# An adaLN gate loaded one group earlier, and its product parted from the residual sum

## The chip, the cores and the metric

The kernel runs on one core of a Trainium2 chip. The metric is the time of one execution on the device in microseconds (us), taken as the median of several runs. Five engines work side by side, each through an instruction list of its own, in order: TensorE (PE, with its weight loads as PEld), VectorE (DVE), ScalarE (ACT), GpSimd (POOL) and SyncE (SP), whose list here issues nearly all DMA transfers. An instruction that needs another engine's result waits on a semaphore, and what stands behind it on its engine waits with it.

## The reference, cut to what matters

Two layers work on 1024 latent tokens of 1024 features; 256 context tokens go through the first layer with the same weights. Everything is float32.

```python
for i in range(DEPTH):                                   # DEPTH = 2
    with_ctx = i < DEPTH - 1
    h, gate_lat = modulate(x, norm_gain[i], cond_lat @ w_mod[i] + b_mod[i])
    hc, gate_ctx = modulate(xc, norm_gain[i], cond_ctx @ w_mod[i] + b_mod[i])
    ...                                                  # h @ w_in[i], four branches: mlp, ret, ga, swa
    if with_ctx:
        xc = xc + gate_ctx * (jnp.concatenate([mlp_c, ret_c, ga_c, swa_c], axis=-1) @ w_out[i])
    x = x + gate_lat * (jnp.concatenate([mlp_l, ret_l, ga_l, swa_l], axis=-1) @ w_out[i])
```

The change concerns the last two lines: the gate is one value per feature, the same for all tokens, and it multiplies the projected result before that is added to `x` or `xc`.

## The kernel before

**Tiling.** The tokens are ten tiles of 128 (eight of latents, two of context, tiles 8 and 9), and two neighbours make a pair: pairs 0 to 3 are latents, pair 4 is context. Weights come in groups of 256 columns: thirteen input groups per layer for the branches (`GROUPS`, the last is `ua1`), then four output groups for the residual. Each operand of these products is held as a rounded high part and a remainder, and a product is three matmuls (`TERMS`). `HT` holds the operand of all ten tiles, eight blocks of 128 features each.

**From branches to projection.** In `ua_group` (L1216) with p = 1, the last branch group, two things fill `HT` for the projection. `stash_mixed` (L1494) loads the stored results of the other branches into room of the attention pool, and `split_mixed` (L1484) turns each tile's part into high part (ACT, L1491) and remainder (L1492, on DVE, or on POOL for blocks 4 to 6 of odd tiles). The group's own result, block 7, goes the same way chunk by chunk (chunks are tiles 0 to 3, 4 to 7, and 8 and 9): two activation steps end in `ge` and `sl` (DVE, each in a `gv` buffer), L1244 multiplies them, POOL multiplies by the stored `svl` (L1249), and a split follows.

**Projection and residual.** `project` (L1533) runs four groups of 256 output columns (n = 0 to 3). For each group it computes one unit per pair (`unit_a`, L418): 48 matmuls over tile and k, the blocks 0 to 7, into one of two PSUM buffers (`pj`). Pairs come in the order 4, 0, 1, 2, 3 in layer 0, and 0 to 3 in layer 1. Behind each unit `residual` (L1583) does three things on DVE and ACT: the gate product `tm` (L1587) from PSUM, the sum into `xr` (L1589), and in layer 0 the squares for the next norm; in layer 1 the sum is stored to the output. `residual` gives back both the PSUM buffer and the `gv` buffer that holds the product.

**The residual's room.** `x` and the gate rows lie in a pool that takes the place of the attention pool. `enter` (L1539) opens it once every buffer of the attention pool is free, that is, behind the last split of the stash; it queues the DMAs: the first 256 columns of the gate and of `x`, and 8 us later by the planner's clock the rest. A gate load (L1552) spreads one row of DRAM over 128 partitions.

**What sets the order.** The instruction lists are written by a planner when the kernel is built (`later`, `hook`, `fits`, L276 to L329). A step is queued with the time at which its inputs should be there by a rough model of the engines; what it needs is a number of buffers by tag and a condition. Whenever the main loop has issued a few matmuls, `hook` runs the steps that are due and fit, earliest first. A step queued by another one is due when the work of that one ends in the model. So the place of an instruction in its engine's list depends on modelled times, on the buffers, and on the condition. The tags that matter are `gv` (4 buffers), `pj` (2) and `vf` (1). `vf` holds the values of an attention group, and in the retention groups `dec`, the decay table (L692), which `Bb1`, the group before `ua1`, reads last (L1401).

The line that ties the product to the pool, in `project`:

```python
self.residual(l, n, pair, tiles, ps, XR[pair], gb[c], None if last else room[pair]), "gv", lambda: XR)
```

Its last argument is the condition: `XR` is an empty list until `enter` has run.

Of the kernel before, what the change touches and what calls it, by code (L numbers as in the profile page):

```python
# [12 lines left out]
F32 = mybir.dt.float32  # L13
# [177 lines left out]
class Program:  # L191
# [161 lines left out]
    def room(self, need):  # L353
        self.until(lambda: self.fits([(need, 1)], None))
# [861 lines left out]
    def ua_group(self, W, p):  # L1216
        V, G, l = self.V, self.G, self.l
        svs = {}

        def load_sv(t0, w):  # L1220
            sv = self.tile(self.gp, (128, 512), F32, "M", "svl")
            self.SP.dma_start(out=sv[:, :w], in_=self.svd[l][p, :, 128 * t0:128 * t0 + w])
            svs[t0] = sv

        if p == 1:
            for ch in self.order():
                t0, n = CHUNKS[ch]
                self.later(lambda t0=t0, w=128 * n: load_sv(t0, w), "M", lambda t0=t0, n=n: all(("v", l, t // 2) in self.made for t in range(t0, t0 + n)))
            stash = self.stash_mixed()
        for ch in self.order():  # L1230
            t0, n = CHUNKS[ch]
            w = 128 * n
            box = {}

            def got(which, a, box=box, t0=t0, n=n, w=w):
                box[which] = a
                if len(box) == 2:
                    if p == 0:
                        self.later(lambda: load_sv(t0, w), "M", lambda: all(("v", l, t // 2) in self.made for t in range(t0, t0 + n)))
                    self.later(lambda: both(box, t0, n, w), "", lambda: t0 in svs)  # L1240

            def both(box, t0, n, w):
                m, g = box["u"], box["g"]
                V.scalar_tensor_tensor(m[:, :w], m[:, :w], 0.25, g[:, :w], ALU.mult, ALU.mult)  # L1244
                self.done(g)
                self.later(lambda: fin(m, svs.pop(t0), t0, n, w))

            def fin(m, sv, t0, n, w):
                G.tensor_mul(m[:, :w], m[:, :w], sv[:, :w])  # L1249
                self.done(sv)  # L1250
                if p == 0:
                    self.later(lambda: self.store_mixed(BLOCKS["A0"], t0, n, m))
                else:
                    def split():
                        self.split_mixed(t0, n, BLOCKS["A1"], 1, m[:, :w].rearrange("p (t k j) -> p t k j", t=n, k=1))
                        self.done(m)
                        self.mixed(t0, n)

                    self.later(split)

            self.gelu2(self.unit_b(W, 0, ch), w, lambda a, got=got: got("u", a))
            self.silu2(self.unit_b(W, 1, ch, ch == 1), w, lambda a, got=got: got("g", a))
            if p == 1:
                for t in range(t0, t0 + n):
                    for k0, nk in ((0, 4), (4, 3)):
                        self.later(lambda t=t, k0=k0, nk=nk: stash[t, k0](), "", lambda t=t, k0=k0: (t, k0) in stash and self.calm())
# [217 lines left out]
    def split_mixed(self, t0, n, k0, nk, src, E=None):  # L1484
# [6 lines left out]
        self.S.activation(hi, src, AF.Copy)  # L1491
        (E or self.V).tensor_sub(lo, src, hi.bitcast(F32))  # L1492

    def stash_mixed(self):  # L1494

        l, stash = self.l, {}
        if self.last:
            parts = [("qkt", 0, 4, (0, 1, 2, 3)), ("PT", 4, 3, (0, 1, 2)), ("PT", 4, 3, (3, 4, 5)), ("qkt", 0, 4, (4, 5, 6, 7)), ("P", 4, 3, (6, 7))]
        else:
            parts = [("qkt", 0, 4, (8, 9, 0, 1, 2)), ("PT", 4, 3, (8, 9, 0)), ("PT", 4, 3, (1, 2, 3)), ("qkt", 0, 4, (3, 4, 5, 6, 7)),  # L1500
                     ("PT", 4, 3, (4, 5, 6)), ("P", 4, 3, (7,))]

        def load(tag, k0, nk, ts):
            m = self.tile(self.ap, (128, len(ts), nk * 128), F32, tag, "mr")
            for a, b in ((0, 2), (2, len(ts))) if ts[0] == 8 else ((0, len(ts)),):
                self.SP.dma_start(out=m[:, a:b, :], in_=self.mxd[l][ts[a]:ts[a] + b - a, :, k0:k0 + nk, :].rearrange("t p k j -> p t (k j)"))
            left = [len(ts)]

            def split(i, t):
                self.split_mixed(t, 1, k0, nk, m[:, i:i + 1, :].rearrange("p t (k j) -> p t k j", k=nk), self.G if k0 and t % 2 else self.V)  # L1510
                left[0] -= 1
                if left[0] == 0:
                    self.done(m)
                self.mixed(t, 1)

            def landed():
                for i, t in enumerate(ts):
                    stash[t, k0] = lambda i=i, t=t: split(i, t)

            self.later(landed)  # L1520

        for tag, k0, nk, ts in parts:
            self.later(lambda tag=tag, k0=k0, nk=nk, ts=ts: load(tag, k0, nk, ts), tag,
                       lambda k0=k0, nk=nk, ts=ts: all((l, t, k) in self.stored for t in ts for k in range(k0, k0 + nk)))
        return stash
# [7 lines left out]
    def project(self, l, x_in):  # L1533
        V, G, SP, A, last = self.V, self.G, self.SP, self.A, self.last
        npair = 4 if last else 5
        XR, gb, room = [], [], [None] * npair
        self.squares = []

        def enter():  # L1539

            rp = self.swap(f"res{l}")
            XR.extend(rp.tile([128, 2, 1024], F32, name=f"xr{l}_{i}") for i in range(npair))
            gb.extend(rp.tile([128, 1024], F32, name=f"gb{l}_{c}") for c in range(1 if last else 2))
            if not last:
                room[:] = [XR[4]] + XR[:3] + [rp.tile([128, 2, 1024], F32, name="xn")]
            self.squares = [rp.tile([128, 8], F32, name=f"sq{l}_{i}") for i in range(0 if last else npair)]
            for fn in first:
                self.later(fn)
            for i, fn in enumerate(rest):
                self.later(fn, wait=8000.0 + 1500 * i)  # L1550

        def load_gate(c, lo, hi):  # L1552
            SP.dma_start(out=gb[c][:, lo:hi], in_=self.gated[l][c:c + 1, lo:hi].to_broadcast([128, hi - lo]))

        def load_x(pair, lo, hi):
            SP.dma_start(out=XR[pair][:, :, lo:hi], in_=x_in(pair)[:, :, lo:hi])


        first, rest = [lambda: load_gate(0, 0, 256)], [lambda: load_gate(0, 256, 1024)]
        if not last:  # L1560
            first.append(lambda: load_gate(1, 0, 256))
            rest.append(lambda: load_gate(1, 256, 1024))
        for pair in range(4) if last else (4, 0, 1, 2, 3):
            first.append(lambda pair=pair: load_x(pair, 0, 256))
            rest.append(lambda pair=pair: load_x(pair, 256, 1024))
        self.normed = self.scaled = 0
        self.later(enter, when=lambda: all(len(self.slots[tag]) == n for tag, n in ATT.items()))
        for n in range(4):
            W = self.next_group()
            for pair in range(4) if last else (4, 0, 1, 2, 3):  # L1570
                c = 0 if pair < 4 else 1
                end = last and n == 3 and pair == npair - 1
                self.until(lambda: min(self.parts[2 * pair:2 * pair + 2]) == 3)
                for tiles in ((0,), (1,)) if end else ((0, 1),):
                    ps = self.unit_a(W, pair, last=pair == 3 and tiles[-1] == 1, tiles=tiles)
                    self.later(lambda n=n, pair=pair, tiles=tiles, ps=ps, c=c:
                               self.residual(l, n, pair, tiles, ps, XR[pair], gb[c], None if last else room[pair]), "gv", lambda: XR)
        if last:
            self.drain()
        else:  # L1580
            self.later(lambda: self.swap(f"att{l + 1}"), when=lambda: self.normed == npair)

    def residual(self, l, n, pair, tiles, ps, xr, gb, room):  # L1583
        m, i = len(tiles), tiles[0]
        tt = self.gv((128, 2, 256), n="tm")
        tm = tt[:, 0:m, :]
        self.V.tensor_mul(tm, ps.rearrange("p (t c) -> p t c", t=2)[:, i:i + m, :], gb[:, 256 * n:256 * n + 256].unsqueeze(1).to_broadcast([128, m, 256]))  # L1587
        xs = xr[:, i:i + m, 256 * n:256 * n + 256]
        (self.V if m == 1 else self.e("res")).tensor_add(xs, xs, tm)  # L1589
        self.done(tt)  # L1590
        self.done(ps)
        o = 256 * pair + 128 * i
        if l == DEPTH - 1:
            self.later(lambda: self.SP.dma_start(
# [182 lines left out]
```

## Time and profile before

| what | value |
|---|---|
| three runs | 1328.32, 1332.09, 1333.88 us |
| median | 1332.09 us |
| profiled execution, its own time | 1333.8 us |
| span in the profile, first to last instruction | 1332.0 us |
| mean granted TensorE clock | 0.983 of full |
| PE busy | 1276.1 us, 96% of the span |
| DVE, ACT, POOL busy | 843.8, 705.3, 610.5 us |

Busy time is averaged over stages that differ. PE is busy nearly throughout, so its gaps matter, and the question is which work ends them. [...]

### The profile page before, as it was taken

What the parts mean: (1) busy time and instruction counts of PE and PEld (TensorE: products, weight loads), DVE (VectorE), ACT (ScalarE), POOL (GpSimd) and SP (SyncE); (2) the same over time, 40 slices, a digit from 0 to 9 for tenths busy, and PEclk for the clock granted to TensorE, in tenths of its full rate; (3) what the DMA queues carried; (4) which work ended last, traced back from release to release, by engine and by line L of the source; (5) the groups of instructions that cost most, each with busy time, mean ns of one, the idle gap of its engine ahead of it and who ended that gap; (6) DMA issues with size and microseconds to landing.
All of it is one profiled execution on the core that took longest, in us unless ns stands there. A gap on an engine that the chain in (4) does not pass through costs nothing. (4 is left out here: it accounts for less than half of the span.)

```text
span 1332.0 us, 27948 instructions
## 1 busy us (share of the span) xinstructions
PE 1276.1 (96%) x10720; PEld 1124.3 (84%) x10720; DVE 843.8 (63%) x2022; ACT 705.3 (53%) x1467; POOL 610.5 (46%) x616
## 2 busy tenths in 40 slices
PE   6989999999999899998999999999999889999998
PEld 3868878889889688887999988789888878788998
DVE  4765878988987652237225766778898884524422
ACT  3556767777776741235224556667788665223300
POOL 2586846735743212324112485768486422223320
PEclk9999999999999999998999999999999989899999
DMA  9436799799798921173411347997988975115521
GB/s 358 155 78 156 139 223 189 149 200 206 148 163 196 189 82 44 45 245 106 164 32 70 124 116 151 186 197 143 187 167 156 199 155 119 28 33 198 201 80 48
DMA packets 373350, 194.13 MB, mean 146 GB/s; under 512 B 303296, under 2 KB 333664, under 8 KB 372192
## 3 DMA queue, kind: packets, MB, share of 16 engines
q1 hardware_dynamic: 373072, 192.28, 61.4%
q8 instruction: 84, 1.38, 0.4%
q14 instruction: 50, 0.41, 0.1%
q10 hardware_dynamic: 144, 0.07, 0.0%
HBM read 94.63 MB, written 23.74 MB: 89 GB/s over the span
## 5 line engine op out<-in xcount | busy, mean ns | idle before, releaser
L429 PE MATMUL ua<-w,HT 128*128 128x256 f32 x4128 | 528.8, 286 | 9.1 <-DVE tm L1587 8.7
L429 PEld LDWEIGHTS ua<-w,HT 128*128 128x128 f32 x4128 | 506.1, 192 | 12.8 <-DVE tm L1587 6.2
L443 PE MATMUL ub<-HT,w 128*128 128x512 f32 (+1 forms) x1824 | 400.4, 373 | 4.4 <-ACT kT L1292 2.1
L443 PEld LDWEIGHTS ub<-HT,w 128*128 128x128 f32 x1824 | 310.3, 192 | 62.3 <-issue 2.9
L372 POOL TENSOR_TENSOR w<-raw,w 128x512 fp32r<-128x512 f32 x132 | 186.0, 1419 | 284.8 <-ACT w L370 259.3
L1032 DVE TENSOR_TENSOR L<-P,H 128x1120 f16<-128x1120 f32 (+2 forms) x104 | 142.3, 1368 | 18.1 <-ACT H L1023 17.8
L370 ACT ACTIVATE w<-raw 128x512 fp32r<-128x512 f32 x136 | 83.5, 626 | 108.0 <-PE ua L429 56.8
L993 DVE CUSTOM_DVE_ANT_0 P<-S,zero 128x512 f32<-128x512 f32 (+2 forms) x216 | 116.2, 582 | 30.1 <-PE S L974 18.8
L974 PE MATMUL S<-qkt 128*128 128x256 f16 (+2 forms) x768 | 125.0, 305 | 3.7 <-DVE mx L993 3.7
L1032 POOL TENSOR_TENSOR L<-P,H 128x160 f16<-128x160 f32 (+2 forms) x104 | 81.0, 780 | 98.8 <-ACT H L1023 65.7
L1023 ACT ACTIVATE H<-P 128x1280 f16<-128x1280 f32 (+2 forms) x104 | 124.7, 1199 | 2.0 <-DMA PT<-H 1.2
L1045 PE MATMUL O<-vh,PT 128*128 128x128 f16 (+1 forms) x1952 | 102.8, 208 | 5.0 <-DVE M L1061 2.4
L1015 ACT ACTIVATE P<-P,mx,gmxC 128x1280 f32<-128x1280 f32 (+1 forms) x72 | 97.6, 1356 | 18.0 <-DVE mx L1002 17.1
L1587 DVE TENSOR_TENSOR tm<-ua,gb 128x512 f32<-128x512 f32 (+1 forms) x37 | 25.0, 676 | 126.8 <-PE ua L429 124.2
L974 PEld LDWEIGHTS <-qkt 128*128 128x128 f16 x768 | 65.1, 99 | 45.0 <-issue 7.6
L1045 PEld LDWEIGHTS <-PT 128*128 128x128 f16 x1952 | 89.2, 99 | 15.2 <-issue 7.0
L573 ACT ACTIVATE ev<-ub 128x512 f32<-128x512 f32 (+1 forms) x64 | 34.7, 542 | 107.7 <-PE ub L443 84.8
L567 POOL TENSOR_TENSOR rr<-rt,mhalf 128x6 f32<-128x6 f32 (+3 forms) x60 | 76.3, 1271 | 5.0
L1015 ACT ACTIVATE P<-P,mx,gmxD 128x640 f32<-128x640 f32 (+2 forms) x72 | 61.6, 855 | 19.6 <-DVE mx L1006 14.5
L1121 DVE SCALAR_TENSOR_TENSOR sl<-th,ev 128x512 f32<-128x512 f32 (+1 forms) x40 | 36.2, 906 | 35.2 <-ACT th L1116 30.4
L993 DVE CUSTOM_DVE_ANT_0 P<-S,mask 128x512 f32<-128x512 f32 (+2 forms) x112 | 50.6, 483 | 7.7 <-PE S L974 5.0
L827 POOL TENSOR_TENSOR rt<-sw,cst 128x192 f32<-128x192 f32 x64 | 48.8, 782 | 3.0 <-ACT sw L833 2.6
(177 smaller groups left out, 1549.0 us busy)
## 6 DMA issues: line engine op xcount, KB each, us to landing
raw<-in_win SPq DMA_DIRECT2D x104, 256.0 KB
raw<-in_wmod SPq DMA_DIRECT2D x64, 256.0 KB
wm<-in_wmod SPq DMA_DIRECT2D x8, 1024.0 KB
raw<-in_wout SPq DMA_DIRECT2D x32, 256.0 KB
xt<-in_x SPq DMA_DIRECT2D x4, 1024.0 KB
silu<-sl SPq DMA_DIRECT2D x16, 256.0 KB
gt<-silu SPq DMA_DIRECT2D x16, 256.0 KB
mxd<-mg SPq DMA_DIRECT2D x16, 256.0 KB
```

The source lines that it names most:

```text
L370: self.S.activation(w[:, :, 0, :], rv, AF.Copy)
L372: self.e(f"w{'i' if o < 0 else 'to'[o > 0]}low{q}").tensor_sub(w[:, :, 1, :], rv, w[:, :, 0, :].bitcast(F32))
L429: self.T.matmul(ps[:, 256 * i:256 * i + 256], self.HT[:, 2 * pair + i, k, sa, :], W[k // 2][:, k % 2, sb, :], start=(j == 0 and n == 0), s ...
L443: self.T.matmul(ps[:, :128 * n], W[k // 2][:, k % 2, sa, 128 * b:128 * b + 128], self.HT[:, t0:t0 + n, k, sb, :], start=(k == 0 and m == 0 ...
L567: self.G.tensor_tensor(r[:, :n], t[:, :n], self.mhalf[:, :n], ALU.pow)
L827: E.tensor_mul(out[:, :, :, 32 * c:32 * c + 32], x[:, :, :, 32 * c:32 * c + 32], t.to_broadcast([128, 2, 3, 32]))
L974: T.matmul(sp[o // 4][:, c:c + 128 * m], qk[:, t, heads[s], :], qk[:, keys[i]:keys[i] + m, b, :], start=(b == 2), stop=(b == 3))
L993: V.tensor_tensor_reduce(out=P[:, 128 * o:128 * (o + m)], in0=sp[o // 4][:, c:c + 128 * m], in1=mk, scale=1.0, scalar=-3e38, op0=ALU.add, ...
L1015: S.activation(P[:, ws * s:ws * s + ws], P[:, ws * s:ws * s + ws], AF.Exp, scale=lc["c"][typ][0], bias=mx[:, s:s + 1], accum_out=sv[:, col ...
L1023: S.activation(H[:, 0:w], P[:, 0:w], AF.Copy)
L1032: E.tensor_sub(L[:, a:b], P[:, a:b], H[:, a:b])
L1045: T.matmul(O[:, 128 * s:128 * s + m], pt[:, pl * len(cols) + j, :], vh()[:, kt, 0:m], start=(j % nk == 0 and pl == 0), stop=(j % nk == nk ...
```

## The change

The first 256 columns of the gate get a tile of their own, `gate0`, in the `vf` room. `first_gate` loads them in the last branch group, once the decay table is done with. `enter` no longer loads them. `residual` now only multiplies; it needs a `gv` buffer and no pool. The sum and what follows become `added`, a step that waits until the planner has seen that pair's first load of `x` land (`there`). The PSUM buffer is given back with the product, the `gv` buffer with the sum.

```diff
             stash = self.stash_mixed()
+            self.later(self.first_gate, "vf")
...
+    def first_gate(self):
+
+        g = self.gate0 = self.tile(self.gp, (128, 2, 256), F32, "vf", "gb")
+        for c in range(1 if self.last else 2):
+            self.SP.dma_start(out=g[:, c, :], in_=self.gated[self.l][c:c + 1, 0:256].to_broadcast([128, 256]))
+
...
+        there = set()
+
         def load_x(pair, lo, hi):
+            if lo == 0:
+                self.later(lambda: there.add(pair))
             SP.dma_start(out=XR[pair][:, :, lo:hi], in_=x_in(pair)[:, :, lo:hi])
 
 
-        first, rest = [lambda: load_gate(0, 0, 256)], [lambda: load_gate(0, 256, 1024)]
+        first, rest = [], [lambda: load_gate(0, 256, 1024)]
         if not last:
-            first.append(lambda: load_gate(1, 0, 256))
             rest.append(lambda: load_gate(1, 256, 1024))
...
                     self.later(lambda n=n, pair=pair, tiles=tiles, ps=ps, c=c:
-                               self.residual(l, n, pair, tiles, ps, XR[pair], gb[c], None if last else room[pair]), "gv", lambda: XR)
+                               self.residual(l, n, pair, tiles, ps, lambda: XR[pair], self.gate0[:, c, :] if n == 0 else gb[c][:, 256 * n:256 * n + 256],
+                                             lambda: None if last else room[pair], lambda: pair in there, n == 0 and pair == 3), "gv")
...
-    def residual(self, l, n, pair, tiles, ps, xr, gb, room):
+    def residual(self, l, n, pair, tiles, ps, xr, gate, room, there, over):
         m, i = len(tiles), tiles[0]
         tt = self.gv((128, 2, 256), n="tm")
         tm = tt[:, 0:m, :]
-        self.V.tensor_mul(tm, ps.rearrange("p (t c) -> p t c", t=2)[:, i:i + m, :], gb[:, 256 * n:256 * n + 256].unsqueeze(1).to_broadcast([128, m, 256]))
+        self.V.tensor_mul(tm, ps.rearrange("p (t c) -> p t c", t=2)[:, i:i + m, :], gate.unsqueeze(1).to_broadcast([128, m, 256]))
+        self.done(ps)
+        if over:
+            self.done(self.gate0)
+        self.later(lambda: self.added(l, n, pair, tiles, tt, xr(), room()), "", there)
+
+    def added(self, l, n, pair, tiles, tt, xr, room):
+        m, i = len(tiles), tiles[0]
+        tm = tt[:, 0:m, :]
         xs = xr[:, i:i + m, 256 * n:256 * n + 256]
         (self.V if m == 1 else self.e("res")).tensor_add(xs, xs, tm)
         self.done(tt)
-        self.done(ps)
```

## Rows read from the trace of the kernel before

**Rows 1.** Waits of PE from 560 us on: in total, times, longest.

```profile
PE ua L429 <- DVE tm L1587: 8.7, 2, 6.0
...
PE pt L608 <- DVE xr L593: 2.0, 1, 2.0
```

**Rows 2.** Windows: length, busy PE, PEld, DVE, ACT, POOL; granted clock; DMA share, GB/s.

```profile
609.50:621.20 11.70, 11.70 (x97) 11.48 (x96) 11.39 (x12) 7.07 (x14) 8.64 (x7) 1.00 0.12 36
621.20:627.20 6.00, 0.04 (x2) 0.02 (x1) 3.37 (x5) 1.04 (x2) 2.37 (x2) 0.75 0.51 122
627.20:640.00 12.80, 12.80 (x92) 12.80 (x93) 3.35 (x5) 2.73 (x12) 0.00 (x0) 0.85 1.02 377
640.00:660.00 20.00, 20.00 (x169) 20.00 (x168) 6.61 (x8) 5.67 (x19) 5.18 (x4) 1.00 0.36 124
740.00:1231.40 491.40, 479.07 (x3970) 411.00 (x3969) 344.88 (x864) 295.86 (x586) 256.61 (x261) 0.98 0.67 142
1231.40:1243.10 11.70, 11.70 (x97) 11.46 (x95) 8.05 (x9) 7.07 (x14) 8.37 (x6) 1.00 0.03 9
1243.10:1245.80 2.70, 0.01 (x1) 0.02 (x1) 2.56 (x4) 1.04 (x2) 1.55 (x2) 0.94 0.06 8
1245.80:1262.00 16.20, 16.19 (x123) 16.20 (x124) 4.75 (x7) 0.63 (x1) 1.44 (x2) 0.90 1.00 349
```

**Rows 3.** Order of time on PE where it goes on after the two stalls.

```profile
627.19 13.00 PE L429 MATMUL ua<-w,HT 128*128 128x256 f32 x92 [5.96 <-DVE tm L1587]
...
1245.81 16.35 PE L429 MATMUL ua<-w,HT 128*128 128x256 f32 x123 [2.71 <-DVE tm L1587]
```

**Rows 4.** Order of time on DVE in layer 0: last split, first product, first sum.

```profile
623.19 0.68 DVE L1492 TENSOR_TENSOR HT<-ge,HT 128x512 fp32r<-128x512 f32 x1
626.44 0.69 DVE L1587 TENSOR_TENSOR tm<-ua,gb 128x512 f32<-128x512 f32 x1 [2.57 <-DMA gb<-gate]
627.19 0.69 DVE L1589 TENSOR_TENSOR xr<-xr,tm 128x512 f32<-128x512 f32 x1
```

**Rows 5.** Order of time on DVE in layer 1, around its stall.

```profile
1239.58 1.51 DVE L1492 TENSOR_TENSOR HT<-mr,HT 128x512 fp32r<-128x512 f32 x1
...
1244.38 0.68 DVE L1492 TENSOR_TENSOR HT<-ge,HT 128x512 fp32r<-128x512 f32 x1
1244.98 0.68 DVE L1587 TENSOR_TENSOR tm<-ua,gb 128x512 f32<-128x512 f32 x1
1247.33 0.69 DVE L1589 TENSOR_TENSOR xr<-xr,tm 128x512 f32<-128x512 f32 x1 [1.67 <-DMA xr<-x]
1247.94 0.68 DVE L1587 TENSOR_TENSOR tm<-ua,gb 128x512 f32<-128x512 f32 x1
```

**Rows 6.** Order of time on SP: what follows the stash loads in each layer.

```profile
578.93 4.65 SPq L508 DMA_DIRECT2D raw<-in_wmod  x4
...
1216.06 0.36 SPq L1106 DMA_DIRECT2D mxd<-ym  x1
```

**Rows 7.** Readers of the decay table, layer 0 and layer 1: first and last start.

```profile
L1401 DVE TENSOR_TENSOR sc<-sc,dec x8: 414/681/692, 523.8 to 570.1; 128x512 f32<-128x512 f32 x6, 128x256 f32<-128x256 f32 x2
...
L1401 DVE TENSOR_TENSOR sc<-sc,dec x6: 674/682/692, 1162.2 to 1200.0; 128x512 f32<-128x512 f32 x6
```

**Rows 8.** Order of time on POOL in layer 1: its splits of odd tiles.

```profile
1237.76 1.48 POOL L1492 TENSOR_TENSOR HT<-mr,HT 128x384 fp32r<-128x384 f32 x1
1239.20 1.34 POOL L1492 TENSOR_TENSOR HT<-mr,HT 128x384 fp32r<-128x384 f32 x1
...
1244.60 1.34 POOL L1492 TENSOR_TENSOR HT<-mr,HT 128x384 fp32r<-128x384 f32 x1 [1.15 <-ACT HT L1491]
```

**Rows 9.** Windows: the slice of layer 1 with the longest idle time of PE.

```profile
1040.00:1060.00 20.00, 16.36 (x170) 14.62 (x168) 18.94 (x67) 15.52 (x36) 5.36 (x7) 0.91 0.93 182
```

**Rows 10.** Order of time on DVE in layer 0's last quarter: one block of the next norm.

```profile
724.66 0.42 DVE L625 CAST HT<-hf 128x512 fp32r<-128x512 f32 x1
725.11 0.69 DVE L626 TENSOR_TENSOR HT<-hf,HT 128x512 fp32r<-128x512 f32 x1
```

## The prediction

> **What bounds the kernel now.** I read the waits of TensorE first, then windows around the longest one, then each engine's order of time inside those windows. Behind the opening, the longest wait of PE is for one instruction, the gate product `tm` of L1587: 8.7 us in two waits [rows 1]. The windows show where: both lie where the output projection takes over from the branch groups, once per layer. In layer 0, PE runs two units (11.70 us, so 5.85 each), stands for 6.0 us and goes on; in layer 1 it runs two units and stands for 2.7 us [rows 2]. The order of time gives 5.96 and 2.71 us and names L1587 both times [rows 3]. The cause is in the code: a unit's result sits in one of two PSUM buffers (`pj`), and a buffer comes free when its product is done. So the third unit waits for the product of the first, and that product may only be issued once `enter` has opened the residual's pool, which is after the last split of HT. In layer 0 it then still waits 2.57 us for its gate rows [rows 4]; in layer 1 it follows the splits at once [rows 5].
>
> Each stall has a second price. [...] At full clock a matmul of this stage costs 20.00/169 = 0.1183 us; 92 of them should take 10.88 us and took 12.80 (1.92 lost), 123 should take 14.55 and took 16.19 (1.64 lost) [rows 2]. PE is otherwise busy in these stages, so the most the change can win here is 5.96 + 1.92 + 2.71 + 1.64 = 12.23 us.
>
> **The change, part by part.** *The gate's first quarter* moves from `enter` into the last branch group. Its two DMAs (one in layer 1) now stand on SP behind the stash loads, before 578.93 in layer 0 and before 1216.06 in layer 1 [rows 6]. They wait for the last reader of the decay table, which starts at 570.1 and 1200.0 [rows 7], earlier than that place, so SP is not held. They push four weight loads (from 578.93) back by two issues, about 0.9 us by the 4.65 us that four took; the last of these waited for POOL anyway, and I cost it at nothing. If that cover is gone, the price is 0.9 us. Both places are some 20 us and more ahead of the first product, so its gate has landed.
>
> *The gate leaves `enter`*, so the x loads are issued one or two places earlier. That helps the sums, not PE.
>
> *Product and sum become two steps.* All products and sums stay. The product no longer waits for the pool, only for a `gv` buffer. Four exist; the last chunk's `ge` and `sl` hold two, so two products can be out early, the number that the first two units need. In layer 0 the first product falls after PE's first unit, at 615.4, and the second after 621.2, so the third unit starts at 621.2 and the fourth at 627.05. What is late next? The fourth unit (tiles 4 and 5) needs the split of the last chunk, which ended at 623.19 + 0.68 = 623.87 [rows 4]. Two products of 0.69 us [rows 4] ahead of it make 625.25, still 1.8 us early. All 5.96 us and the 1.92 us of clock go.
>
> In layer 1 the third unit would start at 1243.1 and reads tiles 4 and 5 itself. Their last split ends at 1244.38 + 0.68 = 1245.06 [rows 5]. Does the unit wait for it at its first matmul? No: the second unit started at 1237.3 and ran without a gap [rows 2] although POOL's share of tile 3 only began at 1237.76 and took 1.48 us [rows 8]. Waits stand at the matmul that reads the piece. The last chunk is block 7, that is k = 7, behind 21 matmuls of tile 4: 1243.1 + 21 x 5.85/48 = 1245.66. A product put into DVE's row earlier delays the split by 0 to 0.69 us, to 1245.06 to 1245.75, and with 0.15 us from DVE's end to PE's start (1245.66 to 1245.81 [rows 3, 5]) PE waits 0 to 0.24 us. I take 0.1: a subtraction on DVE that started at 1239.58 beside a POOL subtraction took 1.51 us, the one at 1244.38, begun before POOL's next, 0.68 [rows 5, 8], and the product at 1244.98 took 0.68 although POOL was at work from 1244.60 [rows 5, 8]. Put ahead of the slow subtraction, the product fills time that DVE lost anyway.
>
> [...]
>
> The fourth unit of layer 1 (from 1248.9) needs the second product. Even behind the first sum, which started at 1247.33, it ends by 1247.33 + 0.69 + 0.69 = 1248.7 [rows 5]: no wait.
>
> **Sum:** 12.23 - 0.1 = 12.1 us off the profiled execution, 1333.8 us (span 1332.0), so 1321.7. That execution is 1.7 us above the median of the three runs, 1332.09; against the median the forecast is 1320.0. No change can be told from one of under 0.5%, 6.7 us.
>
> **The rivals.** *Only layer 0 wins* (0.16). For: DVE is busy 2.56 of the 2.70 us of that wait [rows 2], and if the unit waits for the whole split at its first matmul, the same DVE work ends the same wait. Against: the unseen wait on tile 3. Price: 5.96 + 1.92 = 7.9 us, 1324.2.
>
> *A sum in DVE's row holds back a product* (0.05). DVE takes its work in order: the second product of layer 1 started at 1247.94, behind a sum that waited 1.67 us for x [rows 5], though its unit was done at 1243.1. If layer 0's first sum (x there by 627.19 [rows 4]) is issued ahead of the second product, that product ends at 627.19 + 2 x 0.69 = 628.57 and PE waits 1.5 us from 627.05; in layer 1 a second sum ahead costs 0.6. Time: 1322.1. [...]
>
> *The order of layer 1 changes* (0.16). The order is made from modelled times, and the change alters DVE's items in layer 0's last quarter. From 740 to 1231.4 PE stands 491.4 - 479.07 = 12.3 us at a clock of 0.98 [rows 2], so stalls there can come or go. One more like the largest 20 us slice, 3.64 us idle with the clock at 0.91 (1.8 us) [rows 9], leaves 12.1 - 5.4 = 6.7: 1325.4, at the edge of no change.
>
> *Slower: the sum is lost behind the next layer's splits* (0.06). In layer 0's fourth quarter, every pair's sum leads to its norm, its transposes and the first units of layer 1, and PE already waits 2.0 us for DVE there [rows 1]. Before, sum followed product at once; now splits that come due in between go first. A pair's four casts and subtractions take 4 x (0.42 + 0.69) = 4.44 us [rows 10]. Four pairs' blocks ahead of the last sum are 17.8 us of PE plus 1.9 of clock, net 7.6 slower: 1339.7. It decides from the third block on (13.3 + 1.9 against 12.1). Against it: steps go by their due time, and a sum is due 0.7 us behind its product.
>
> *It does not do what it says* (0.05): were no `gv` buffer free, products would come when they do now: 1332.
>
> **How the numbers follow.** Forecast 0.52, rivals 0.16, 0.05, 0.16, 0.06, 0.05. Faster by over 0.5% are the forecast, the first two rivals and a fifth of the third: 0.52 + 0.16 + 0.05 + 0.03 = 0.76. Within 0.5%: 0.13 + 0.05 = 0.18. Slower: 0.06. The range starts at 1315, the forecast with one such layer 1 stall fewer (5.4 us), and ends at 1328, the third rival with 2.6 us more for the spread of the runs; the last two rivals stay outside.
>
> **What would show it.** Right: no PE wait on L1587 in either stage, the first products at about 615 and 1240, a granted clock of 1.00 from 600 to 730, the third unit without a gap to the second. Wrong: a wait of PE for an HT split in layer 1's stage, a new wait where layer 1 begins, or sums far behind their products.

## The result, and the profile after

The changed kernel took 1314.95 us (median of six runs, 1312.24 to 1318.18), the kernel before 1331.76 us (six runs, 1328.32 to 1333.88): a ratio of 0.9878, 95% interval 0.9858 to 0.9898. A second comparison, below, gave 1318.71 against 1328.68 us, 0.9915 (0.9888 to 0.9942). The gain is 16.8 us in the one and 10.0 us in the other.

| what | before | after |
|---|---|---|
| profiled execution, its own time | 1333.8 us | 1318.18 us |
| span, first to last instruction | 1332.0 us | 1316.4 us |
| PE busy | 1276.1 us, 96% | 1272.4 us, 97% |
| mean granted TensorE clock | 0.983 | 0.987 |

The waits of PE from 560 us on, in the kernel after (in total, times, longest):

```profile
PE S L974 <- DVE mx L993: 4.1, 5, 2.1
PE O L1045 <- DVE M L1061: 3.1, 2, 1.6
PE vx L887 <- DVE vm L881: 1.4, 1, 1.4
```

The wait for `tm`, 8.7 us in two [rows 1], is gone. So is the one of 2.0 us for `xr` (rows that DVE scales for the next norm and PE then turns), and in its place stands a new one of 1.4 us for `vm` (the largest attention value of each partition, found by DVE). The order of time of PE in the two projections, after:

```profile
607.98 33.28 PE L429 MATMUL ua<-w,HT 128*128 128x256 f32 x276
...
1220.10 31.16 PE L429 MATMUL ua<-w,HT 128*128 128x256 f32 x258
```

Each is one group without a bracket (brackets hold the idle time ahead of an instruction and what ended it): PE goes through more than five units of 5.85 us with no idle time, where before it stood 5.96 and 2.71 us ahead of the third [rows 3]. The windows, cut as in [rows 2] and moved by the start of each stage (length; busy PE, PEld, DVE, ACT, POOL; granted clock as a share of full speed; DMA share, GB/s), with one over all of layer 0's projection ahead of them:

```profile
600.00:730.00 130.00, 130.00 (x1057) 128.60 (x1057) 60.64 (x87) 45.55 (x132) 38.94 (x33) 1.00 0.33 113
...
621.20:627.20 6.00, 6.00 (x53) 6.00 (x52) 3.72 (x5) 1.82 (x8) 0.67 (x1) 1.00 0.53 157
627.20:640.00 12.80, 12.80 (x109) 12.80 (x108) 3.28 (x5) 2.23 (x9) 1.29 (x1) 1.00 1.01 376
...
1231.80:1234.50 2.70, 2.70 (x25) 2.70 (x25) 1.91 (x3) 1.05 (x2) 1.54 (x2) 1.00 0.03 4
1234.50:1250.00 15.50, 15.50 (x131) 15.50 (x130) 5.49 (x9) 0.63 (x1) 1.40 (x2) 1.00 0.98 350
```

PE is busy for all of 130.00 us from 600 to 730, at a clock of 1.00. The clock is 1.00 in the other four too, and 12.80 us hold 109 matmuls where they held 92 at a clock of 0.85 [rows 2]. What DVE does around them, in order of time, layer 0 and then layer 1:

```profile
614.81 0.68 DVE L1598 TENSOR_TENSOR tm<-ua,gb 128x512 f32<-128x512 f32 x1
...
619.85 0.68 DVE L1598 TENSOR_TENSOR tm<-ua,gb 128x512 f32<-128x512 f32 x1
...
622.35 0.68 DVE L1493 TENSOR_TENSOR HT<-ge,HT 128x512 fp32r<-128x512 f32 x1
622.95 0.68 DVE L1608 TENSOR_TENSOR xr<-xr,tm 128x512 f32<-128x512 f32 x1
625.40 0.69 DVE L1608 TENSOR_TENSOR xr<-xr,tm 128x512 f32<-128x512 f32 x1 [1.77 <-DMA xr<-in_x]
626.01 0.68 DVE L1598 TENSOR_TENSOR tm<-ua,gb 128x512 f32<-128x512 f32 x1
...
1228.23 0.68 DVE L1598 TENSOR_TENSOR tm<-ua,gb 128x512 f32<-128x512 f32 x1
1228.83 0.91 DVE L1493 TENSOR_TENSOR HT<-mr,HT 128x512 fp32r<-128x512 f32 x1
...
1233.03 0.68 DVE L1493 TENSOR_TENSOR HT<-ge,HT 128x512 fp32r<-128x512 f32 x1
1235.97 0.69 DVE L1608 TENSOR_TENSOR xr<-xr,tm 128x512 f32<-128x512 f32 x1 [2.26 <-DMA xr<-x]
1236.58 0.68 DVE L1598 TENSOR_TENSOR tm<-ua,gb 128x512 f32<-128x512 f32 x1
```

Products now stand among the splits (L1493), ahead of the last split; two of the sums (L1608) wait for `x`, and PE does not wait for them.

**Where the time came from.** To read this run by run, I cut every profiled execution at four instructions of PE's order of time: the first unit of layer 0's projection, the first `ub` matmul of layer 1, its first `O` matmul, and the first unit of layer 1's projection. (`ub` are projections of the branch groups, `O` is attention output; from the second cut to the third, layer 0's last units and layer 1's first ones overlap, and I call that stretch the seam.) The table has the lengths between them, in us, for all kernels of the study; the experiments use it.

| kernel | up to projection 0 | layer 0's projection | seam, to the first `O` | layer 1, to projection 1 | layer 1's projection | span |
|---|---|---|---|---|---|---|
| before | 609.55 | 126.60 | 83.89 | 411.39 | 100.57 | 1332.0 |
| after | 607.98 | 118.67 | 81.43 | 412.02 | 96.30 | 1316.4 |
| layer 0 alone | 604.86 | 118.68 | 83.85 | 411.19 | 100.62 | 1319.2 |
| layer 1 alone | 605.98 | 126.12 | 83.95 | 412.11 | 96.24 | 1324.4 |
| first quarter alone | 607.62 | 118.69 | 83.60 | 406.85 | 96.24 | 1313.0 |
| later sums apart alone | 607.41 | 126.72 | 81.88 | 411.58 | 99.21 | 1326.8 |
| gate early alone | 608.64 | 123.03 | 83.75 | 406.46 | 99.12 | 1321.0 |
| fillers in the stalls | 608.56 | 124.48 | 84.27 | 405.36 | 99.13 | 1321.8 |
| after, block 7 first | 606.56 | 118.68 | 81.50 | 407.99 | 99.77 | 1314.5 |
| after, again | 609.84 | 118.67 | 81.50 | 410.98 | 96.31 | 1317.3 |
| seam alone | 609.08 | 126.75 | 81.46 | 410.92 | 100.49 | 1328.7 |
| after, seam joined | 607.59 | 118.68 | 83.65 | 409.06 | 96.22 | 1315.2 |

Before minus after: 1.57 + 7.93 + 2.46 - 0.63 + 4.27 = 15.6 us of span. The two projections give 12.20, the seam 2.46. The first and fourth columns differ as much among kernels with the same work: "after" and "after, again" are the same program and differ by 1.86 and 1.04 us there, but by 0.07 us at most in the other three columns. The fourth goes with the clock: of its longest and its shortest, "layer 1 alone" has a granted clock of 0.97 there and PE busy for 402.27 us, "fillers" 0.99 and 395.30, while PE's idle time is 9.84 and 10.06 us.

### The profile page after: what moved, and what is told of

Its sections match the earlier page's. It is cut to its first block, busy times and chain, and to the rows that moved or that the text cites. A ratio compares the mean times of both kernels' runs of the same rounds, so it can differ in the third digit from the quotient of the medians.

```text
span 1316.4 us, 27946 instructions
## 1 busy us (share of the span) xinstructions
PE 1272.4 (97%) x10720; PEld 1121.9 (85%) x10720; DVE 841.8 (64%) x2022; ACT 703.4 (53%) x1467; POOL 610.6 (46%) x616
## 4 chain that ended last, share of the span: by engine, by line
PE 79%; DVE 9%; POOL 3%; ACT 3%; issue 3%; DMA 3%; SPq 1%; POOLq 0%; ACTq 0%; DVEq 0%
PE ua L429 32%; PE ub L443 26%; PE S L974 6%; PE O L1045 5%; DVE P L993 2%; PE y L1418 2%; PE y L1414 2%; PE mod L520 1%; POOL rr L567 1%; DMA xt<-in_x 1%; PE u L1714 1%; PE kvp L1330 1%; PE sc L1386 1%; DVE qr L827 1%; DVE L L1032 1%
## 5 line engine op out<-in xcount | busy, mean ns | idle before, releaser
L1032 DVE TENSOR_TENSOR L<-P,H 128x1120 f16<-128x1120 f32 (+2 forms) x104 | 143.1, 1376 | 18.2 <-ACT H L1023 16.8
```

The lines of the kernel that those rows point to most:

```text
L1032: E.tensor_sub(L[:, a:b], P[:, a:b], H[:, a:b])
```

## The experiments

The variants of the change are the changed kernel with two sets: in which layers the gate loads early, and in which quarters (layer, n) product and sum are two steps. All times are medians; the ratios are to the kernel before, run on the same chip.

**Layer 0 alone.**

```diff
+EARLY = {0}
+PART = {(0, 0)}
...
-            self.later(self.first_gate, "vf")
+            if l in EARLY:
+                self.later(self.first_gate, "vf")
...
-                               ... lambda: pair in there, n == 0 and pair == 3), "gv")
+                               ... lambda: pair in there, early and n == 0 and pair == 3),
+                               "gv", None if early and (l, n) in PART else lambda: XR)
...
-        self.later(lambda: self.added(l, n, pair, tiles, tt, xr(), room()), "", there)
+        if (l, n) in PART:
+            self.later(lambda: self.added(l, n, pair, tiles, tt, xr(), room()), "", there)
+        else:
+            self.added(l, n, pair, tiles, tt, xr(), room())
```

> The change in layer 0's first quarter alone: gate early, product apart from the sum for n = 0; layer 1 and the other quarters as before. Theory (the gain is the two PE stalls with the clock behind them): 5.96 + 1.92 = 7.9 us less, ratio 0.994; PE runs without a gap from 609 to 735, the stall of 2.71 us in layer 1 and the wait of about 2 us where layer 1 begins stay. Rival (the new order of the last branch group is worth something of its own): up to 1.6 us more, 9.5 us less, ratio 0.993.

Measured: 1319.88 against 1330.18 us, 0.9936 (0.9912 to 0.9959). Its longest waits for product and sum:

```profile
PE ua L431 <- DVE tm L1605: 2.7, 1, 2.7
PE pt L610 <- DVE xr L595: 2.0, 1, 2.0
```

Of the two waits for the product one is left, layer 1's. Layer 0's projection takes 118.68 us, as in the whole change: 7.92 us less than before.

**Layer 1 alone.**

```diff
+EARLY = {1}
+PART = {(1, 0)}
```

> The change in layer 1's first quarter alone; layer 0 and the sums of the other quarters as before. Theory: 2.71 + 1.62 - 0.1 = 4.2 us less, ratio 0.997; layer 0's stall of 6 us stays. Rival (layer 1's third unit waits for the last split as a whole, so its stall only stays because of layer 0): no change, ratio 1.000.

Measured: 1323.83 us, 0.9965 (0.9948 to 0.9981). One wait for the product is left, of 5.7 us; layer 1's projection takes 96.24 us, 4.33 less than before. So the third unit of layer 1 does not wait for the whole split, and the rival "only layer 0 wins" falls.

**First quarter alone**: both layers, without the parted sums of the later quarters.

```diff
+EARLY = {0, 1}
+PART = {(0, 0), (1, 0)}
```

> Gate early and product apart in both layers, but only for n = 0; for n = 1 to 3 the sum follows its product at once, as before. Theory: the sum of the two, 12.1 us less, ratio 0.991, and the wait of about 2 us where layer 1 begins is still there. Rival (all of the change's 16 us belongs to the two stalls): 16 us less, ratio 0.988.

Measured: 1314.75 us, 0.9894 (0.9873 to 0.9915). By the time alone this lies between the two expectations. By the stages it has the whole gain of both projections (118.69 and 96.24 us) and none of the seam's (83.60).

**Later sums apart alone**: the gate as before, product and sum two steps in quarters 1 to 3.

```diff
+EARLY = set()
+PART = {(l, n) for l in (0, 1) for n in (1, 2, 3)}
```

> Only the sums of n = 1 to 3 are steps of their own; gate and first quarter as before. Theory: the order where layer 1 begins becomes that of the changed kernel, its PE wait of 1.96 us goes, with up to 1.3 us of clock (3 us at 0.56): 2.0 to 3.3 us less, ratio 0.998. Rival (the surplus is scatter of the clock): no change, ratio 1.000.

Measured: 1327.65 us, 0.9983 (0.9963 to 1.0004), which does not tell the two expectations apart. The waits do:

```profile
PE ua L431 <- DVE tm L1605: 8.3, 2, 5.7
...
PE vx L889 <- DVE vm L883: 1.4, 1, 1.4
```

Both waits for the product stay, the wait for `xr` is gone and the one for `vm` is there. So these two differences of the change come from the parted sums and not from the gate. Two later kernels ask which quarter.

**Gate early alone**: the first quarter's gate in its own tile in both layers, product and sum one step that waits for the pool.

```diff
+EARLY = {0, 1}
+PART = set()
```

> Only the gate is loaded early; product and sum stay together and wait for the pool. Theory (in layer 0 the gate's load ends the wait, behind it the pool): the product can run when the splits end, 623.9 instead of 626.44, so 2.5 us of layer 0's stall go, and of the clock 0 to 1.9 us; layer 1 keeps its 2.7 us. 2.5 to 4.4 us less, ratio 0.997 to 0.998. Rival (the gate is the whole of it in layer 0): 7.9 us less, ratio 0.994.

Measured: 1323.85 against 1329.92 us, 0.9961 (0.9945 to 0.9978). The order of time of PE, where it goes on after the two stalls:

```profile
622.91 19.27 PE L431 MATMUL ua<-w,HT 128*128 128x256 f32 x146 [2.59 <-DVE tm L1605]
...
1236.23 18.95 PE L431 MATMUL ua<-w,HT 128*128 128x256 f32 x156 [2.68 <-DVE tm L1605]
```

The early gate takes 5.96 - 2.59 = 3.37 us of standing from layer 0 and nothing from layer 1. What is left in both is the wait for the pool; the step that does not need it takes that.

**Fillers in the stalls**: the kernel before, with matmuls on PE that nobody reads where it stands, 45 in layer 0 and 18 in layer 1. The question is whether the slow restart is a second price or would have come anyway.

```diff
+                    if n == 0 and pair == (2 if last else 1):
+                        self.fill(W, 18 if last else 45, 0 if last else 8)
                     ps = self.unit_a(W, pair, last=pair == 3 and tiles[-1] == 1, tiles=tiles)
...
+    def fill(self, W, count, t):
+        self.room("pm")
+        ps = self.pm("fill")
+        for _ in range(count):
+            self.T.matmul(ps[:, 0:256], self.HT[:, t, 0, 0, :], W[0][:, 0, 0, :], start=True, stop=True)
+        self.done(ps)
```

> The kernel before, with 45 matmuls in layer 0 and 18 in layer 1 put on PE where it stood (5.3 and 2.1 us of them, into a PSUM buffer that nobody reads). The waits stay as long; PE is merely at work in them. Theory (the restart at half clock comes from standing): granted clock 1.00 through both stages, 1.92 + 1.62 = 3.5 us less, ratio 0.997. Rival (the clock falls at the start of the projection whatever PE does): no change or some tenths slower, ratio 1.000.

Measured: 1324.3 us, 0.9968 (0.9951 to 0.9985): faster, with more work. The fillers in the order of time, and the windows over and behind them:

```profile
620.07 5.56 PE L1589 MATMUL fill<-w,HT 128*128 128x256 f32 x45
625.77 16.46 PE L429 MATMUL ua<-w,HT 128*128 128x256 f32 x135
...
1234.18 2.32 PE L1589 MATMUL fill<-w,HT 128*128 128x256 f32 x18
1237.04 17.15 PE L429 MATMUL ua<-w,HT 128*128 128x256 f32 x141 [0.53 <-DVE tm L1596]
```

```profile
620.00:627.00 7.00, 6.86 (x57) 6.66 (x57) 5.04 (x6) 1.10 (x4) 2.55 (x2) 1.00 0.44 135
627.00:640.00 13.00, 13.00 (x110) 13.00 (x110) 4.10 (x7) 3.24 (x15) 0.27 (x1) 1.00 1.01 370
1234.00:1237.00 3.00, 2.50 (x21) 2.30 (x20) 2.89 (x4) 1.05 (x2) 1.84 (x2) 1.00 0.05 4
1237.00:1253.00 16.00, 15.96 (x133) 15.99 (x134) 4.75 (x7) 0.63 (x1) 1.45 (x2) 1.00 1.00 347
```

The third unit begins 17.21 us after the first in layer 0 (625.77 - 608.56) and 14.37 us in layer 1 (1237.04 - 1222.67), against 17.64 and 14.38 before (627.19 - 609.55, 1245.81 - 1231.43 [rows 3]): the fillers only fill the wait. But PE now stands for 0.14 and 0.50 us in the windows over it, and the clock stays at 1.00. Layer 0's projection gets 126.60 - 124.48 = 2.12 us shorter, 0.43 of it by the shorter wait and 1.69 by the clock (1.92 was the term of the sum); layer 1's 1.44 (the term was 1.64). In layer 1 one execution does not show that the fillers did it: "later sums apart" and "gate early" take 99.21 and 99.12 us there without them.

**After, with block 7 first.** The third unit of layer 1 reads k = 7 first instead of last, so that its first matmul needs the last split.

```diff
...
-        steps = [(i, k) for k in range(KT) for i in tiles] if last else [(i, k) for i in tiles for k in range(KT)]
+        ks = (7, 0, 1, 2, 3, 4, 5, 6) if early else range(KT)
+        steps = [(i, k) for k in range(KT) for i in tiles] if last else [(i, k) for i in tiles for k in ks]
...
```

> The changed kernel, with block 7 (the one split last) first instead of last in layer 1's third unit. Theory (the wait for a split stands at the matmul that reads it, and its place at k = 7 hid it): the unit starts 0.15 us behind the end of that split, a PE wait of 2.0 us, and 0 to 1.6 us of clock; 2.0 to 3.6 us slower than the changed kernel. Rival (the split is there in time for the unit's first matmul anyway): as the changed kernel, 0.988 of the one before.

Measured: 1320.04 us, 0.9935 (0.991 to 0.996), against 0.9878 and 0.9915 for the change. The order of time of PE, and the last split on DVE:

```profile
1227.43 0.50 PE L430 MATMUL ua<-w,HT 128*128 128x256 f32 x2 [1.03 <-ACT HT L1493]
1228.39 33.80 PE L430 MATMUL ua<-w,HT 128*128 128x256 f32 x267 [0.46 <-DVE HT L1494]
```

```profile
1227.66 0.68 DVE L1494 TENSOR_TENSOR HT<-ge,HT 128x512 fp32r<-128x512 f32 x1
```

PE waits 1.03 + 0.46 = 1.49 us and goes on within 0.05 us of the split's end (1228.34). The projection takes 99.77 us, 3.47 more than in the change: 1.49 is that wait, and most of the rest the clock, 0.90 over the 16.00 us from 1229.00 on (124 matmuls). The wait stands at the matmul that reads the block, as the prediction took it from the unseen wait on tile 3, and k = 7 coming last is what lets layer 1 win the whole of its wait.

**After again, seam alone, seam joined.** These ask what the parted sums bring, and whether the 16.8 us repeat. The first is the changed kernel itself, the second parts only layer 0's last quarter, the third joins only that quarter.

```diff
+EARLY = set()
+PART = {(0, 3)}
```

```diff
+EARLY = {0, 1}
+PART = {(l, n) for l in (0, 1) for n in range(4)} - {(0, 3)}
```

> The changed kernel itself, on the same chip as the next two. Both theories: no wait of PE for the gate product, about 107.5 us from the third unit's stage... counted from the first unit of layer 0's projection to layer 1's first products about 118.7 us (before 126.6), and 96.3 us from layer 1's first unit to the end if the clock holds (before 100.6), so about 12.2 us off the two stages. If what the time gained over these 12.2 us is the seam alone (1.96 us of standing and 1.7 us of clock), the ratio is 0.988 to 0.989. If the surplus was the chance of the clock in the stretches with unchanged order, the ratio falls back to 0.991.

> The kernel before, with product and sum as two steps in layer 0's last quarter only. If that alone reorders the work where layer 1 begins, the 2.0 us wait of PE for the sum there is gone and both long waits for the gate product stay: 2 us of standing, and up to 1.7 us of clock with it, so a ratio of 0.997 to 0.9985 against before. If the reordering only moves the wait, the ratio is 1.000.

> The changed kernel, with product and sum as one step again in layer 0's last quarter only. If that quarter alone makes the seam, the 2.0 us wait of PE for the sum is back and both long waits for the product stay away: 2 to 3.7 us slower than the change on the same chip, ratio to before 0.990 to 0.992. If the parted sums bring nothing there, the ratio equals the change's own.

Measured, against 1328.68 us: again 1318.71 us, 0.9915 (0.9888 to 0.9942); seam alone 1326.71 us, 0.998 (0.9964 to 0.9996); seam joined 1317.88 us, 0.991 (0.9885 to 0.9936). The interval of "again" reaches both expectations, and that the joined seam came out 0.83 us below the whole change, not 2 us above it, shows only that medians with a scatter of 10 us (1310.67 to 1320.68) cannot weigh this part. With the later sums parted the ratios are 0.9878 and 0.9915, without 0.9894 ("first quarter alone") and 0.991. The stages can: the column of the seam is 81.43 to 81.88 us in the five kernels that part layer 0's last quarter and 83.60 to 84.27 in the seven that don't. The order of time there, of "after, seam joined" and then of "seam alone":

```profile
747.48 2.27 PE L610 MATMUL pt<-cst,xr 128*128 128x128 f32 x15 [1.96 <-DVE xr L595]
```

```profile
772.25 0.49 PE L889 MATMUL vx<-cst,vm 128*128 128x128 f32 x2 [1.37 <-DVE vm L883]
```

Layer 0's last quarter is the only one that matters: "later sums apart", which parts six quarters, and "seam alone", which parts this one, have the same instructions in the same order on PE, DVE, ACT and POOL. The wait for `xr` goes because DVE ends the last scaling (L593) 18.7 us behind the seam's start in the kernel after (744.64 + 0.75 - 726.65) and 21.2 us before (756.57 + 0.75 - 736.15).

One wait took the place of another, 1.37 us for 1.96. That is 0.59 of the 2.46 us between before and after; the rest is PE's busy time, at another clock. The windows of PE alone over the first 30 us of the seam, before and after (length, busy PE, granted clock, DMA share, GB/s):

```profile
736.15:766.15 30.00, 27.95 (x222) 0.94 0.33 105
```

```profile
726.65:756.65 30.00, 29.88 (x255) 1.00 0.23 74
```

Behind the standing of 1.96 us the clock falls, behind the 1.37 us in "after" it does not (1.00 from 756.65 to 786.65). But the gain does not hang on the clock. "Fillers" parts nothing, and its seam ran at 1.00 (28 us busy of the first 30); it was not shorter for it, but the longest of all, 84.27 us. There the wait for `xr` stands and one for `vm` comes as well:

```profile
754.24 1.86 PE L608 MATMUL pt<-cst,xr 128*128 128x128 f32 x15 [1.95 <-DVE xr L593]
...
771.54 0.49 PE L887 MATMUL vx<-cst,vm 128*128 128x128 f32 x2 [1.11 <-DVE vm L881]
```

In the kernel before, the slow stretch behind the first wait hid the second: PE comes to `vx` 38.8 us into the seam there without a wait, and 38.5 us into it in "fillers" with one. By this one execution the parting is worth some 2.1 to 2.8 us at a clock of 1.00 (84.27, of which 0.28 us is a wait for weights that no other kernel has there, against 81.43 to 81.88).

## Why the prediction was right, and where it was short

**The cause and the two stalls.** Right, step by step. The first products came at 614.81 and 1228.23 us, 6.8 and 8.1 us into their stages; 615.4 and 1240 was forecast, 5.9 and 8.6 us into those of before. The forecast was 7.88 us for layer 0's stage and 4.25 for layer 1's with the 0.1 of waiting taken off; the stages gave 7.93 and 4.27, and the two experiments on one layer 7.92 and 4.33. The early gate and the product that does not need the pool are both needed in layer 0 (3.57 us of 7.9 come from the gate alone), and only the second in layer 1.

**The clock as a second price.** Right in layer 0: six kernels without the stall take 118.67 to 118.69 us there, and the fillers give back 1.69 us beyond what their wait was shorter by. Behind both stalls of the kernel before the granted clock is 0.50 and then 1.00:

```profile
627.20:631.00 3.80, 3.80 (x18) 3.80 (x19) 1.97 (x3) 1.82 (x8) 0.00 (x0) 0.50 1.01 307
631.20:640.00 8.80, 8.80 (x75) 8.80 (x75) 1.38 (x2) 0.91 (x4) 0.00 (x0) 1.00 1.03 406
1245.81:1248.80 2.99, 2.99 (x14) 2.99 (x15) 1.43 (x3) 0.00 (x0) 0.13 (x1) 0.50 0.88 269
1249.00:1262.00 13.00, 13.00 (x110) 13.00 (x109) 3.12 (x5) 0.63 (x1) 1.30 (x1) 1.00 1.03 369
```

3.80 us at half the clock lose 1.90 us of the 1.92, 2.99 us 1.50 of the 1.64. In layer 1 it is a price that is paid only sometimes. "Later sums apart" and "gate early" stand there for 2.7 us like the kernel before and "seam alone", yet take 99.2 and 99.1 us where those take 100.6 and 100.5. Windows over and behind this stall, first of "later sums apart", then of "seam alone":

```profile
1239.27:1241.97 2.70, 0.02 (x1) 0.05 (x1) 2.53 (x4) 1.04 (x2) 1.54 (x2) 1.00 0.07 14
1241.97:1258.17 16.20, 16.20 (x135) 16.20 (x136) 4.75 (x7) 0.63 (x1) 1.39 (x2) 1.00 0.99 351
```

```profile
1239.90:1242.60 2.70, 0.03 (x1) 0.06 (x1) 2.53 (x4) 1.04 (x2) 1.55 (x2) 0.91 0.04 13
1242.60:1258.80 16.20, 16.20 (x124) 16.20 (x125) 4.75 (x7) 0.63 (x1) 1.39 (x2) 0.91 0.99 348
```

The same wait with the same neighbours costs 1.3 us of clock (100.49 against 99.21) in one and none in the other. The 1.64 us of the sum were right for the execution that was read, and are not owed in every one: against the two kernels that stood there at a clock of 1.00, the change's 96.30 us are only 2.8 to 2.9 us less.

**Product and split in layer 1.** The 0.1 us of waiting did not come. The last split ends 13.61 us after the stage begins (1233.03 + 0.68 - 1220.10), against 13.63 before (1245.06 - 1231.43), with a product ahead of it: the product was free. It took its 0.68 us while POOL subtracted, and the subtraction behind it took 0.91 us where it had taken 1.51 [rows 5]. POOL at that time:

```profile
1226.42 2.77 POOL L1493 TENSOR_TENSOR HT<-mr,HT 128x384 fp32r<-128x384 f32 x2
```

It ends at 1229.19, and the subtraction of DVE 0.55 us later (1228.83 + 0.91 = 1229.74). Before, POOL ended at 1239.20 + 1.34 = 1240.54 [rows 8] and the subtraction at 1239.58 + 1.51 = 1241.09 [rows 5], also 0.55 us later. Before, it began 0.96 us ahead of that end (1240.54 - 1239.58), after, 0.36 us (1229.19 - 1228.83): in both kernels it ends by POOL's end and not by its own start. Why a subtraction takes longer beside POOL and the product does not, no run shows; that the product cost nothing is the 13.61 us against 13.63.

**What the sum left out.** The step that failed is "All products and sums stay", with the parted sums of the later quarters costed at nothing; only layer 0's last quarter has a price, and it is a gain. The prediction had the seam's 2.0 us wait in view and asked of it, in the rival on the last quarter, only whether it could grow; that a stall near there could also go is in the rival on layer 1's order and in the range's start, but not in the sum. It shrank. That is 2.46 us in the profiles compared, 2.0 us in the medians of "seam alone". The three stages come to 7.93 + 2.46 + 4.27 = 14.7 us, between the two comparisons (16.8 and 10.0 us). What the comparisons differ by beyond that lies in the stretches that the change does not touch: with nearly the same instructions, the first took 604.86 to 609.84 us and the fourth 405.36 to 412.11 over the twelve kernels. So the first median came out 0.05 us under the range's lower end of 1315; the second, set against the 1332.09 us of the prediction, is 0.9915 x 1332.09 = 1320.8, within 1 us of the forecast. That closeness is chance: the stages of that execution, too, are 7.93 + 2.39 + 4.26 = 14.6 us shorter than before, not 12.1.

**The rivals.** A sum did hold back a product: in layer 0 the product at 626.01 stood behind a sum that waited 1.77 us for `x`. It was the third and not the second, and the unit that needs its buffer comes at 631.4 (607.98 + 4 x 5.85), so nobody waited. In layer 1 the second product ended at 1236.58 + 0.68 = 1237.26, 0.4 us ahead of the fourth unit (1220.10 + 3 x 5.85 = 1237.65); the prediction had 0.2. The order of layer 1 changed at the seam only, and to the better: from the first `O` to layer 1's projection all four engines have the same order of instructions before and after. The sums of the last quarter were not lost behind splits: parting them gave 2.46 us, where that rival had a loss, 7.6 us net. Two of the prediction's signs of being wrong did come, without harm to the total: the wait for `vm` is a new one where layer 1 begins, in place of a longer one, and the first sums stand 5.6 to 8.1 us behind their products (622.95 - 614.81, 625.40 - 619.85, 1235.97 - 1228.23).

**The gate's move.** Two issues, 0.97 us together, now stand ahead of the weight loads on SP, about the 0.9 us named, and no wait of PE for them appears:

```profile
578.77 0.97 SPq L1499 DMA_DIRECT2D gb<-gate  x2
579.84 2.16 SPq L508 DMA_DIRECT2D raw<-in_wmod  x4
```

## What to carry to other kernels

Where a double-buffered result waits for its reader, ask which of the reader's inputs is really late, and part the reader there: here the product needed 256 columns of gate and the sum needed `x`, and only the sum could wait at no cost. Price a stall of PE with the slow restart behind it (1.69 us behind the stall of 5.96 us here), but look at several executions before counting the restart behind a short one as owed. And when a step is cut in two in every pass of a loop, follow each pass whose result the next stage waits for: the cut reorders that seam as well, for better or worse.

## What the runs showed of the hardware that was not expected

After the same standing of 2.7 us, in two programs with the same order of instructions throughout ("later sums apart" and "seam alone"), the granted clock was 0.91 in one execution and 1.00 in the other. With the fillers, the seam's standing of 1.95 us also left it at 1.00 over 30 us (0.94 in the kernel before). The clock also falls where PE hardly stands (no wait over 0.3 us in the first of these lines, 0.7 in the second): two executions of programs whose instructions agree up to layer 1's projection, "after" and "after, block 7 first", differ over the 80 us that begin 400 us behind the seam's start, at the same busy time of PE (length, busy PE, granted clock, DMA share, GB/s):

```profile
1126.65:1206.65 80.00, 79.12 (x503) 0.91 0.26 81
```

```profile
1125.24:1205.24 80.00, 78.99 (x509) 0.96 0.29 90
```

One execution of a kernel differs from the next along with it: the six of "after, again" go from 1310.67 us at a mean granted clock of 0.995 to 1320.68 us at 0.985. That is why a part worth 2 us was read from its stage and not from the medians. What makes the clock fall in one execution and not in the next stays open.
